# A hybrid mLSTM/GLA decoder block on one Trainium2 core: selectors made a head ahead, two products of a pair exchanged after plain units, a weights' cast behind two bank copies, a last norm in three vector steps

## The chip, the core and the metric

The kernel runs on one core of one Trainium2 chip. The metric is the device time of one execution in microseconds (us). TensorE (PE) multiplies, VectorE (DVE) and ScalarE (ACT) do the elementwise work, GpSimd (POOL) issues accumulating DMAs and SyncE (SP) most of the other DMAs. Each engine works through a list of its own, in the order in which the program wrote it; semaphores hold an instruction until what it reads, or the buffer that it writes, is ready.

## The reference

The input is x (512 tokens, width 1024), ahead of which 16 meta tokens are put. Cut to what matters:

```python
xn = rmsnorm(h, norm1_g)
(mq, mk, mv, mi, mf, mo, gq, gk, gv, ga, gr, gate_m, gate_g) = split_cols(xn @ w_in)
mq, mk = split(silu(causal_depthwise_conv(concat(mq, mk))))       # width 4
# mLSTM, 4 heads: wts = exp(dmat - m_row) * (q k^T);  dmat from sums of log gates
hm = (wts @ v) / maximum(abs(sum(wts)), exp(-m_row))
y_m = head_rmsnorm(hm) * sigmoid(mo)
y_g = head_rmsnorm(gla(gq, gk, gv, log_sigmoid(ga @ g_a2))) * silu(gr)
merged = sigmoid(gate_m) * (y_m @ w_branch_m) + sigmoid(gate_g) * (y_g @ w_branch_g)
h = h + merged @ w_out
hn = rmsnorm(h, norm2_g)
h = h + (silu(hn @ w_ff_gate) * (hn @ w_ff_up)) @ w_ff_down
out = rmsnorm(h, final_g)
```

## The kernel before

**Units.** Activations are held transposed, features on the 128 partitions and tokens along a row. The weights are cut into units of 128 output features. Every float32 operand is split into a high part, a cast (weights: `whi`, on ACT, L190), and the rest (`wlo`, on DVE, L195), and a product takes three matmuls: high by high, high by low, low by high (L304, L305, L306 in `mm3`). A plain unit has 8 steps (k) of three matmuls for each bank of PSUM; there are eight banks, which go round.

**Mixed pairs.** Most of the units are computed two at a time with seven half-size products in place of eight (a Strassen-Winograd scheme; `pair` and `seven`, matmuls L346 to L348, 12 for a product). A pair accumulates in three banks, bx, by and bz. Product p7 goes to bz; q1 goes to bx and q6 is added on top of it, then come p4, p2 and q5, and p3 is left pending into the next pair. `sink_of` names the copies that ACT makes in between: s1 copies what bx holds after q1 (before: L406), s7 copies bz after p7 (L409), s2 copies bx after q6 (L407), L408 is a copy of a pair before it. q6 writes bx, so its first matmul can't start until s1 has read it.

**Tables.** The casts for later units are hooked to steps of a unit or pair: `PLAIN`, `FIRST` (the first of two items that a pair makes) and `SECOND`. An entry such as `("q1", 2)` means: after step 2 of q1.

**The order around the units.** The program is written in one order, by hand: after each step of a unit (every second step of a product) `tick()` lets the generators that wait in `side` and the first one of `mixers` go on by one step; `yield n` makes a generator wait n ticks. The four mLSTM heads (`mlstm`) are such generators, in `mixers`, one after the other. A head begins with a selector, `sel`, a 128x256 cast of constants (L883), waits 6 ticks, and multiplies its two halves with the gate rows `gts.R` (L886, L887). The results are copied and masked (L890 and L891), ACT takes exponentials (L134, in `act`), and for each of five chunks PE makes the scores (L908 to L910), DVE multiplies them with the exponentials (L915), ACT casts the product (`wh`, L919) and DVE keeps the rest (`wl`, L928). Then come sums with the values (L950 to L956) and the head's norm (`head_out`).

**Where things meet.** The units of the four heads come first (gates, then mq, mk, mv, mo for each head, all plain; convolutions of mq and mk run on DVE and ACT beside them). Head 0's selector is made while the convolutions of head 1's mq and mk are under way. The first mixed pair is that of gm units 0 and 1, behind the last mo unit. Two other pairs follow plain units: that of gq and gk of head 1 behind the bm units, and the first fg/fu pair behind six plain fg and fu units. `mixed_x` makes the sums of activations that the pairs need (L546, L551, L582) ahead of the first pair.

**The end.** `final` makes the last norm of each half of the tokens: a sum of squares over the features by a matmul with ones (L1495), `y` = exp(-0.5 ln(...)) on ACT, and one Newton step for it on DVE (L1501 to L1504).

Of the kernel before, what the change touches and what calls it, by code (L numbers as in the profile page):

```python
# [9 lines left out]
F32R = mybir.dt.float32r  # L10
I32 = mybir.dt.int32
AF = mybir.ActivationFunctionType
ALU = mybir.AluOpType
PSUM = bass.MemoryType.PSUM

P = 128
D = 1024
KT = 8
NM = 16
NS = 512  # L20
NT = NM + NS
HALF = NT // 2
H = 4
DFF = 2816
FT = DFF // P
EPS = 1e-6
# [76 lines left out]
def hybrid_block(ctx: ExitStack, tc: tile.TileContext, xT, wst, par, con, out):  # L103
# [5 lines left out]
    def nm(s):  # L109
        cnt[0] += 1  # L110
        return f"{s}_{cnt[0]}"
# [6 lines left out]
    def tt(dt=F32, n=NT, p=P):  # L118
        t = tpool.tile([P, TW], dt, tag="t", name=nm("t"))
        return t[:p, :n]  # L120
# [7 lines left out]
    def act(o, i, func, **kw):  # L128
        want = TABLE.get(func)
        if want is not None and table[0] not in want:  # L130
            table[0] = want[0]
            if func != AF.Silu:
                S.preload_act_table_set(want[0])
        S.activation(o, i, func, **kw)  # L134
# [122 lines left out]
    def g_lo(u):  # L257
# [6 lines left out]

    PLAIN = {"s": [(split_hi, 2), (split_lo, 4)], "e": [(e_hi, 1), (e_lo, 3), (s2, 4)],
             "a": [(a_hi, 1), (a_lo, 3), (f_hi, 4), (s4, 5)]}
    FIRST = {"s": [(split_hi, ("q1", 2)), (split_lo, ("p3", 1))],
             "e": [(e_hi, ("q1", 2)), (e_lo, ("p3", 1)), (s2, ("q6", 1))]}
    SECOND = {"s": [(split_hi, ("p2", 0)), (split_lo, ("p2", 2))],
              "a": [(a_hi, ("p2", 0)), (a_lo, ("p2", 2)), (f_hi, ("q5", 0)), (s4, ("q5", 2))],  # L270
              "e": [(e_hi, ("p2", 0)), (e_lo, ("p2", 2)), (s2, ("q5", 2))]}
# [22 lines left out]
    pend = {}  # L294
# [45 lines left out]
    def seven(o, w, x, n, start, hook, c0, c1):  # L340

        wh, wl = w[n]
        xh_, xl_ = x[n]
        for k in range(4):
            h, l = wh[:, k * P:(k + 1) * P], wl[:, k * P:(k + 1) * P]
            T.matmul(o, h, xh_[k][:, c0:c1], start=start and k == 0, stop=False, skip_group_check=not start)  # L346
            T.matmul(o, h, xl_[k][:, c0:c1], start=False, stop=False, skip_group_check=not start)  # L347
            T.matmul(o, l, xh_[k][:, c0:c1], start=False, stop=k == 3, skip_group_check=not start)  # L348
            hook(n, k)

    def pair(names, x, cols, sink):


        u, steps = begin(*names)
        w = mixw[u].w
        bz, bx, by = (bank()[:, :cols[1] - cols[0]] for _ in range(3))
        e = sink(bz, bx, by)
        todo = {("p7", 0): ["s5"], ("p7", 2): ["mid", "c22"], ("q6", 0): ["c12"], ("q6", 2): ["fin"]}
        mine = {("p3", 0): ["s1", "s7"], ("p4", 0): ["s2"], ("p2", 1): ["c21"], ("q5", 0): ["c11"]}
        steps.setdefault(("p7", 3), []).append(lambda: f_lo(u))  # L360
        steps.setdefault(("q6", 1), []).append(lambda: g_hi(u))
        steps.setdefault(("p4", 1), []).append(lambda: g_lo(u))

        def hook(n, k):
            left(*todo.get((n, k), ()))
            for s in mine.get((n, k), ()):
                e.pop(s)()
            for f in steps.get((n, k), ()):
                f()
            if k % 2:  # L370
                tick()

        seven(bz, w, x, "p7", True, hook, *cols)
        seven(bx, w, x, "q1", True, hook, *cols)
        if "p3" in pend:
            pend.pop("p3")(hook)
        else:
            for k in range(4):
                hook("p3", k)
        seven(bx, w, x, "q6", False, hook, *cols)  # L380
        seven(bz, w, x, "p4", False, hook, *cols)
        seven(by, w, x, "p2", True, hook, *cols)
        seven(bx, w, x, "q5", False, hook, *cols)
        assert not pend, pend
        pend.update(e)
        pend["p3"] = lambda hook=lambda n, k: None: seven(bx, mixw.pop(u).w, x, "p3", False, hook, *cols)
# [36 lines left out]
    for k in range(KT):  # L423
        t = tt()
# [201 lines left out]
    gts = Box()  # L626
    gts.ready = False

    def gate_rows(ps):
        a2s = gts.a2s = apool.tile([P, 512], F32R, name="a2s")  # L630
        a2f = pr[:, C_A2:C_A2 + 512]
        gsb = tt()
        for a in range(2):
            c = slice(a * HALF, (a + 1) * HALF)
            V.tensor_tensor(gsb[:96, c], ps[0][a][:96], rstd[:96, c], ALU.mult)
        yield 16
        gam = gts.gam = tt(F32R)
        S.copy(gam[:96], gsb[:96])
        bi = pr[0:32, C_BG:C_BG + 1]
        bf = pr[32:64, C_BG:C_BG + 1]  # L640
        r1, r2, bl, a0 = tt(p=32), tt(p=32), tt(p=32), tt(p=32)
        act(r1, gsb[32:64], AF.Abs, bias=bf)
        yield 1
        act(r1, r1, AF.Exp, scale=-1.0)
        V.tensor_scalar(r2, gsb[32:64], bf, 0.0, op0=ALU.add, op1=ALU.min)
        yield 1
        act(r1, r1, AF.Ln, bias=b_one[:32])
        V.tensor_tensor(gam[64:96], gsb[64:96], gam[64:96].bitcast(F32), ALU.subtract)
        S.copy(a2s[:96], a2f[:96])
        yield 1  # L650
        V.tensor_tensor(r2, r2, r1, ALU.subtract)
        V.tensor_tensor_scan(bl, rmask[:32], r2, 0.0, ALU.mult, ALU.add)
        yield 1
        V.tensor_tensor(a2s[32:64], a2f[32:64], a2s[32:64].bitcast(F32), ALU.subtract)
        V.scalar_tensor_tensor(a0, gsb[0:32], bi, bl, ALU.add, ALU.subtract)
        yield 1
        d0, ml = r1, r2
        V.memset(d0, 0.0)
        V.tensor_copy(d0[:, CH::CH], bl[:, CH - 1:NT - 1:CH])
        V.tensor_tensor_scan(ml, d0, a0, 0.0, ALU.add, ALU.max)  # L660
        yield 1
        R = gts.R = tt(F32R, NS)
        mr = tt(p=32)
        rhi = d0
        act(R[0:32], ml[:, NM:], AF.Copy, scale=-1.0)
        V.tensor_tensor(mr, ml, bl, ALU.add)
        V.tensor_scalar(mr, mr, -1.0, 40.0, op0=ALU.mult, op1=ALU.min)
        yield 1
        V.scalar_tensor_tensor(R[32:64], ml[:, NM:], -1.0, R[0:32].bitcast(F32), ALU.mult, ALU.subtract)
        S.copy(R[64:96], mr[:, NM:])  # L670
        yield 1
        S.copy(rhi[:, NM:], R[64:96].bitcast(F32))
        yield 1
        V.tensor_tensor(R[96:128], mr[:, NM:], rhi[:, NM:], ALU.subtract)

        acol = gts.acol = apool.tile([P, 480], F32, name="acol")
        gts.idx = {}
        rows = [a0]
        n_ix = 0
        for d in range(NCK):  # L680
            if d > 0:
                nxt = tt(p=32)
                for i in range(NCK - d):
                    e = CH * (i + d) - 1
                    V.tensor_scalar(nxt[:, CH * i:CH * i + CH], rows[-1][:, CH * i:CH * i + CH], bl[:, e:e + 1],
                                    None, op0=ALU.add)
                rows.append(nxt)
            yield 2
        yield 8
        pst = bank()  # L690
        for d in range(NCK):
            n_ix = gate_cols(pst, rows, d, n_ix)
            yield 1
        yield 2
        V.tensor_copy(acol, pst[:, :480])
        gts.ready = True
# [178 lines left out]
    WTOT = off  # L875


    def mlstm(h, q, k, v, gates, dst):
        while not gts.ready or q.v is None or k.v is None:
            yield 1  # L880
        (qh, ql), (kh, kl) = q.v, k.v
        sel = mpool.tile([P, 2, P], F32R, tag="sel", name=nm("sel"))
        S.copy(sel, cn[:, NS + h:NS + 8:H].unsqueeze(2).to_broadcast([P, 2, P]))  # L883
        yield 6
        pb, pm = bank(), bank()
        T.matmul(pb, sel[:, 0], gts.R, start=True, stop=True)  # L886
        T.matmul(pm, sel[:, 1], gts.R, start=True, stop=True)  # L887
        yield 1
        nml, dia, em = tt(n=NS), tt(n=NS), tt(n=NS)
        S.copy(nml, pb)  # L890
        V.tensor_tensor(dia, pb, mask, ALU.add)  # L891
# [595 lines left out]
    def final(a, o):  # L1487
        yield 16
        ps = bank()[:, :HS]
        T.matmul(ps, ones, hsum[a].v, start=True, stop=False)  # L1490
        while o.v is None:
            yield 1
        yield from out_res(7, o.v, a * HS, (a + 1) * HS)
        yield 1
        T.matmul(ps, ones, hsum[a].w, start=False, stop=True)  # L1495
        yield 1
        y, t = tt(n=HS), tt(n=HS)
        act(y, ps, AF.Ln, bias=b_eps, scale=1.0 / D)
        act(y, y, AF.Exp, scale=-0.5)
        yield 1  # L1500
        V.tensor_tensor(t, y, y, ALU.mult)  # L1501
        V.scalar_tensor_tensor(t, ps, D * EPS, t, ALU.add, ALU.mult)
        V.tensor_scalar(t, t, -0.5 / D, 1.5, op0=ALU.mult, op1=ALU.add)
        V.tensor_tensor(y, y, t, ALU.mult)  # L1504
        yield 1
        for j in range(4):
            g = hgain[j, a]
            V.tensor_tensor(g, g, y.unsqueeze(1).to_broadcast([P, 2, HS]), ALU.mult)
            q = S if j % 2 else nc.sync
            q.dma_start(out[2 * j:2 * j + 2, :, a * HS:(a + 1) * HS].rearrange("m p n -> p m n"), g)  # L1510
            yield 1
# [110 lines left out]
```

## Time and profile before

| what | value |
|---|---|
| time, median of 3 runs | 942.75 us (942.73 to 942.78) |
| the profiled execution, its own time | 943.2 us |
| its span in the trace | 941.1 us (2.1 us lie around it) |
| TensorE (PE) busy | 917.7 us |
| VectorE (DVE) busy | 641.0 us |
| ScalarE (ACT) busy | 536.7 us |
| GpSimd (POOL) busy | 86.5 us |
| mean granted TensorE clock | 0.993 of full speed |

Busy times come from the profiled execution, whose own time is 0.45 us above the median of the runs. Matmuls overlap, so that the distance between two starts, not a matmul's own duration, is what it costs PE; the same holds to a smaller part for DVE and ACT.

### The profile page before, as it was taken

To read this page: it belongs to the slowest core of one execution; us is meant where nothing else is said; L and a number is where in the kernel's file an instruction comes from. 1 tells how busy PE (TensorE), PEld (TensorE's weight loads), DVE (VectorE), ACT (ScalarE), POOL (GpSimd) and SP (SyncE) were. 2 spreads that over 40 slices of the span, in tenths; PEclk is the share of its full clock that TensorE was granted. 3 is DMA by queue.
4 is the path that set the end of the run, shared out by engine and by line. 5 is a ranking of instruction groups with operands and counts; after the bars stand their busy time and mean duration, and the time that the engine had idled before them with its cause. 6 is when DMAs were issued, how large, how long until landed. Compare 5 with 4: busy or idle time off the path is not lost.

```text
span 941.1 us, 15476 instructions
## 1 busy us (share of the span) xinstructions
PE 917.7 (98%) x6083; PEld 843.0 (90%) x6083; DVE 641.0 (68%) x948; ACT 536.7 (57%) x947; POOL 86.5 (9%) x102
## 2 busy tenths in 40 slices
PE   6999999989999999999999999999999999999995
PEld 6989999989998899999998888888999999888885
DVE  6898776877865477777777556886767677832323
ACT  7556678779674266767774234443555555732321
POOL 0000022011100011111000000212111210000000
PEclk9999999999999999999999999999999999999998
DMA  6345465355752466565553344244887775332302
GB/s 255 111 132 164 136 141 134 71 125 123 173 143 88 114 152 163 135 139 141 134 137 90 114 141 131 86 124 116 196 187 186 190 179 148 113 108 70 112 1 89
DMA packets 48713, 124.45 MB, mean 132 GB/s; under 512 B 5377, under 2 KB 11521, under 8 KB 48641
## 3 DMA queue, kind: packets, MB, share of 16 engines
q1 hardware_dynamic: 35008, 101.32, 34.6%
q0 software_dynamic: 12544, 21.11, 14.5%
q8 instruction: 47, 0.77, 0.3%
q10 hardware_dynamic: 1088, 1.05, 0.3%
q14 instruction: 26, 0.20, 0.1%
HBM read 118.08 MB, written 5.37 MB: 131 GB/s over the span
## 4 chain that ended last, share of the span: by engine, by line
PE 88%; DVE 5%; ACT 5%; issue 1%; DMA 1%; SPq 0%; DVEq 0%; ACTq 0%
PE b L305 14%; PE b L304 14%; PE b L306 14%; PE b L346 12%; PE b L348 12%; PE b L347 12%; ACT t L134 2%; ACT whi L190 1%; DVE wlo L195 1%; PE b L1069 1%; PE b L1071 1%; PE b L1048 1%; DMA t<-xT 1%; PE b L753 1%; PE b L951 1%
## 5 line engine op out<-in xcount | busy, mean ns | idle before, releaser
L305 PE MATMUL b<-t,whi 128*128 128x512 f32 (+2 forms) x822 | 290.8, 354 | 1.1 <-DVE t L473 0.7
L304 PE MATMUL b<-t,whi 128*128 128x512 f32 (+2 forms) x774 | 274.6, 355 | 6.6 <-ACT t L134 6.6
L306 PE MATMUL b<-t,wlo 128*128 128x512 f32 (+2 forms) x774 | 271.6, 351 | 0.0
L346 PE MATMUL b<-t,whi 128*128 128x256 f32 (+1 forms) x864 | 249.6, 289 | 3.5 <-ACT t L406 2.8
L348 PE MATMUL b<-t,wlo 128*128 128x256 f32 (+1 forms) x864 | 245.3, 284 | 0.0
L347 PE MATMUL b<-t,whi 128*128 128x256 f32 (+1 forms) x864 | 244.5, 283 | 0.0
L195 DVE TENSOR_TENSOR wlo<-raw,whi 128x1024 fp32r<-128x1024 f32 x155 | 193.3, 1250 | 46.2 <-ACT whi L190 45.5
L190 ACT CAST whi<-raw 128x1024 fp32r<-128x1024 f32 x155 | 161.4, 1045 | 62.3 <-PE b L347 26.0
L305 PEld LDWEIGHTS b<-t,whi 128*128 128x128 f32 x822 | 156.4, 190 | 23.7 <-DVE t L473 1.3
L304 PEld LDWEIGHTS b<-t,whi 128*128 128x128 f32 x774 | 147.7, 191 | 26.6 <-ACT t L134 6.6
L346 PEld LDWEIGHTS b<-t,whi 128*128 128x128 f32 x864 | 164.0, 190 | 5.3 <-ACT t L406 3.8
L306 PEld LDWEIGHTS b<-t,wlo 128*128 128x128 f32 x774 | 147.3, 190 | 19.9 <-DVE wlo L195 0.3
L347 PEld LDWEIGHTS b<-t,whi 128*128 128x128 f32 x864 | 163.9, 190 | 0.4
L348 PEld LDWEIGHTS b<-t,wlo 128*128 128x128 f32 x864 | 163.7, 189 | 0.0
L134 ACT ACTIVATE t<-t 128x512 f32<-128x512 f32 (+6 forms) x140 | 80.5, 593 | 58.9 <-DVE t L1098 27.7
L185 POOL DMA_DIRECT2D raw<-wst x36 | 31.1, 864 | 358.2 <-DMA wf<-wst 86.6
L190 ACT CAST whi<-wf 128x1024 fp32r<-128x1024 f32 x36 | 37.8, 1051 | 22.6 <-PE b L347 13.5
L134 ACT ACTIVATE t<-f 128x256 f32<-128x256 f32 (+1 forms) x24 | 11.6, 482 | 61.9 <-DVE f L1469 61.9
L214 POOL DMA_DIRECT2D wf<-wst x36 | 32.1, 901 | 157.2 <-DMA wf<-wst 116.0
L195 DVE TENSOR_TENSOR wlo<-wf,whi 128x1024 fp32r<-128x1024 f32 x36 | 43.8, 1218 | 0.0
L1469 DVE TENSOR_TENSOR f<-f,b 128x512 f32<-128x512 f32 (+1 forms) x9 | 5.6, 628 | 53.6 <-PE b L306 53.6
L346 PE MATMUL b<-t,wgh 128*128 128x256 f32 (+1 forms) x144 | 40.9, 284 | 0.0
(221 smaller groups left out, 1200.6 us busy)
## 6 DMA issues: line engine op xcount, KB each, us to landing
raw<-wst SPq DMA_DIRECT2D x155, 512.0 KB, 3.7
wf<-wst SPq DMA_DIRECT2D x36, 256.0 KB, 3.2
wf<-wst POOLq DMA_DIRECT2D x36, 256.0 KB, 5.6
raw<-wst POOLq DMA_DIRECT2D x36, 256.0 KB, 4.8
t<-xT SPq DMA_DIRECT2D x8, 264.0 KB, 6.1
pos<-t SPq DMA_DIRECT2D x8, 264.0 KB, 2.5
t<-xT SPq DMA_DIRECT2D x8, 256.0 KB, 3.9
t<-neg POOLq DMA_DIRECT2D x6, 272.0 KB, 6.3
```

The costliest lines, as they stand in the source:

```text
L134: S.activation(o, i, func, **kw)
L185: G.dma_start(lr(r, 0), lr(wst[v - 1], 0), accum_op=ALU.add)
L190: S.copy(t, src)
L195: V.tensor_tensor(t, src, hi.bitcast(F32), ALU.subtract)
L214: G.dma_start(lr(st.f, 1), lr(wst[u + 1], 1), accum_op=ALU.add)
L304: T.matmul(o, w_h, ah[:, c0:c1], start=first, stop=False)
L305: T.matmul(o, w_h, al[:, c0:c1], start=False, stop=False)
L306: T.matmul(o, w_l, ah[:, c0:c1], start=False, stop=last)
L346: T.matmul(o, h, xh_[k][:, c0:c1], start=start and k == 0, stop=False, skip_group_check=not start)
L347: T.matmul(o, h, xl_[k][:, c0:c1], start=False, stop=False, skip_group_check=not start)
L348: T.matmul(o, l, xh_[k][:, c0:c1], start=False, stop=k == 3, skip_group_check=not start)
L753: T.transpose(pb[:, c * P:(c + 1) * P], f[:, c * CH:(c + 1) * CH], ident)
```

## The change

Four edits.

- **Selectors.** Each head's selector is made ahead: head 0's at the end of the gate rows, the next head's right behind the two matmuls of the head before it, in one buffer. The wait of 6 ticks is gone.
- **Order of p7 and q1.** Where a pair follows plain units, and no p3 is pending, q1 comes ahead of p7. There are three such pairs.
- **FIRST.** The cast `whi` moves from step 2 of q1 to step 0 of the place of p3, behind s1 and s7; `wlo` moves from step 1 of p3 to step 3, and the sum s2 from step 1 to step 2 of q6. It concerns 36 pairs.
- **The last norm.** The sum's affine part, `x`, is computed beside ACT's two steps; three DVE steps follow in place of four.

```diff
-    FIRST = {"s": [(split_hi, ("q1", 2)), (split_lo, ("p3", 1))],
-             "e": [(e_hi, ("q1", 2)), (e_lo, ("p3", 1)), (s2, ("q6", 1))]}
+    FIRST = {"s": [(split_hi, ("p3", 0)), (split_lo, ("p3", 3))],
+             "e": [(e_hi, ("p3", 0)), (e_lo, ("p3", 3)), (s2, ("q6", 2))]}
...
-        seven(bz, w, x, "p7", True, hook, *cols)
-        seven(bx, w, x, "q1", True, hook, *cols)
+
+        for b, n in ((bz, "p7"), (bx, "q1")) if "p3" in pend else ((bx, "q1"), (bz, "p7")):
+            seven(b, w, x, n, True, hook, *cols)
...
         V.tensor_tensor(R[96:128], mr[:, NM:], rhi[:, NM:], ALU.subtract)
+        selector(0)
...
+    def selector(h):
+        gts.sel = mpool.tile([P, 2, P], F32R, tag="sel", name=nm("sel"), bufs=1)
+        S.copy(gts.sel, cn[:, NS + h:NS + 8:H].unsqueeze(2).to_broadcast([P, 2, P]))
+
     def mlstm(h, q, k, v, gates, dst):
...
-        sel = mpool.tile([P, 2, P], F32R, tag="sel", name=nm("sel"))
-        S.copy(sel, cn[:, NS + h:NS + 8:H].unsqueeze(2).to_broadcast([P, 2, P]))
-        yield 6
+        sel = gts.sel
         pb, pm = bank(), bank()
         T.matmul(pb, sel[:, 0], gts.R, start=True, stop=True)
         T.matmul(pm, sel[:, 1], gts.R, start=True, stop=True)
         yield 1
+        del sel
+        if h < H - 1:
+            selector(h + 1)
...
-        y, t = tt(n=HS), tt(n=HS)
+        y, t, x = tt(n=HS), tt(n=HS), tt(n=HS)
         act(y, ps, AF.Ln, bias=b_eps, scale=1.0 / D)
+        V.tensor_scalar(x, ps, D * EPS, -0.5 / D, op0=ALU.add, op1=ALU.mult)
         act(y, y, AF.Exp, scale=-0.5)
         yield 1
         V.tensor_tensor(t, y, y, ALU.mult)
-        V.scalar_tensor_tensor(t, ps, D * EPS, t, ALU.add, ALU.mult)
-        V.tensor_scalar(t, t, -0.5 / D, 1.5, op0=ALU.mult, op1=ALU.add)
-        V.tensor_tensor(y, y, t, ALU.mult)
+        V.tensor_tensor(t, t, x, ALU.mult)
+        V.scalar_tensor_tensor(y, t, 1.5, y, ALU.add, ALU.mult)
```

The lines of the changed kernel are shifted: its selector cast is L882, the two matmuls L890 and L891, their copy L897, the scores L915 to L917, `wh` L926, and s1, s2 and s7 are L407, L408 and L410.

**ACT at head 0.** The first fence shows ACT's list before, the second the same stretch now, the third where the first selector's cast went. `whi` is a weights' cast, L513 (now L514) the high part of an activation, L134 an activation function, `sel` the selector.

```order
L134 ACTIVATE t_787<-t_777,pr 128x512
L190 CAST whi_796<-raw_625 128x1024
L513 CAST t_799<-t_775 128x528
L134 ACTIVATE t_802<-t_775 128x272
L883 CAST sel_807<-cn 128x256
L757 CAST t_835<-b_824 128x512
```

```order
L134 ACTIVATE t_789<-t_779,pr 128x512
L190 CAST whi_798<-raw_627 128x1024
L514 CAST t_801<-t_777 128x528
L134 ACTIVATE t_804<-t_777 128x272
L882 CAST sel_820<-cn 128x256
L897 COPY t_822<-b_809 128x512
L134 ACTIVATE t_824<-b_810,cb 128x512
```

```order
L134 ACTIVATE t_552<-t_487 32x512
L671 CAST t_552<-t_553 32x512
L673 COPY t_486<-t_552 32x512
L882 CAST sel_581<-cn 128x256
L190 CAST whi_587<-raw_401 128x1024
```

In the place of head 0's selector now stands that of head 1, and the copies of head 0's two products (L897 and the L134 on bank 810) come directly behind it. The first selector stands 17 rows earlier.

**ACT at the first mixed pair.** The first fence is ACT's list before, around the pair's s1 and s7 (L406, L409); the second is the list now, where they are L407 and L410. `acol` marks the exponentials of head 3, `wh` its casts; the operands `b_` are banks.

```order
L890 COPY t_2347<-b_2337 128x512
L190 CAST whi_2356<-raw_2141 128x1024
L134 ACTIVATE t_2349<-b_2338,cb 128x512
L406 COPY t_2311<-b_2307 128x256
L409 COPY t_2312<-b_2306 128x256
L134 ACTIVATE t_2372<-t_2348,acol 128x112
L134 ACTIVATE t_2372<-t_2347,acol 128x128 x2
```

```order
L926 CAST wh_2196<-t_2301 128x272
L134 ACTIVATE t_2338<-t_2174,acol 128x16
L759 CAST t_2359<-b_2346 128x512
L134 ACTIVATE t_2373<-t_2175,acol 128x16
L926 CAST wh_2196<-t_2338 128x144
L776 CAST t_1800<-b_2379 128x256
L133 ACT_TABLE_LOAD
L134 ACTIVATE t_2400<-b_2213 128x512
L134 ACTIVATE t_2401<-b_2304 128x512
L926 CAST wh_2196<-t_2373 128x16
L407 COPY t_2391<-b_2387 128x256
L410 COPY t_2392<-b_2386 128x256
```

Before, head 3 had only its two products behind it when s1 came, and all of its exponentials and `wh` casts stood behind s7. Now the whole of them stand ahead of s1: L897 of head 3 is ACT's row 223, s1 is row 268, and the 44 rows between hold head 3's exponentials, all five `wh` casts, two table loads, three weights' casts and the casts and copies of `mixed_x`. The weights' cast L190 that stood ahead of s1 stands behind L410.

**PE at the first mixed pair.** The fence shows three places of PE's list now: the pair's beginning, the step from q1 to p7, and the step from p7 to q6. Bank 2387 is bx, 2386 is bz.

```order
L773 MATMUL b_2379<-pr,t_2220 128x128
L346 MATMUL b_2387<-t_2265,whi_2318 128x256
...
L348 MATMUL b_2387<-t_2269,wlo_2330 128x256
L346 MATMUL b_2386<-t_1806,whi_2228 128x256
...
L348 MATMUL b_2386<-t_1810,wlo_2249 128x256
L346 MATMUL b_2387<-t_1996,whi_2344 128x256
```

Before, the pair began with p7 into bz, and q1 into bx stood directly ahead of q6, with three score matmuls of head 3 between. Now the 12 matmuls of p7 lie between q1 and q6, and the two selector matmuls of head 3, which stood behind the pair's p7 at row 1195, stand at row 1107, 95 rows ahead of the pair.

## Rows read from the trace of the kernel before

**Rows 1.** The page: busy time, share of the span and instructions.

```profile
PE 917.7 (98%) x6083; PEld 843.0 (90%) x6083; DVE 641.0 (68%) x948; ACT 536.7 (57%) x947; POOL 86.5 (9%) x102
```

**Rows 2.** The list of PE's waits: total, times, longest, in us.

```profile
PE b L346 <- ACT t L406: 2.8, 2, 2.3
PE b L886 <- ACT sel L883: 2.2, 1, 2.2
...
PE b L346 <- ACT t L1391: 0.5, 1, 0.5
```

**Rows 3.** Timeline of ACT at head 0's selector: start, duration, line, operation, idle before.

```profile
67.78 0.81 ACT L134 ACTIVATE t<-t,pr 128x512 f32<-128x512 f32 x1 [0.89 <-DVE t L595]
68.50 1.03 ACT L190 CAST whi<-raw 128x1024 fp32r<-128x1024 f32 x1
...
70.30 0.39 ACT L883 CAST sel<-cn 128x256 fp32r<-128x256 f32 x1
```

**Rows 4.** Timeline of PE at the same place.

```profile
70.74 0.50 PE L886 MATMUL b<-t,sel 128*128 128x512 f32 x1 [2.21 <-ACT sel L883]
```

**Rows 5.** Windows behind two waits: busy by engine (PE, PEld, DVE, ACT, POOL), then granted clock.

```profile
71.00:75.00 4.00, 4.00 (x20) 3.91 (x20) 4.00 (x8) 0.44 (x2) 0.00 (x0) 0.57 0.53 166
211.00:215.00 4.00, 4.00 (x22) 4.00 (x22) 3.56 (x7) 3.63 (x8) 0.87 (x1) 0.57 0.56 111
```

**Rows 6.** Timeline of PE: q6 of the second pair, and of the first fg/fu pair.

```profile
209.86 0.39 PE L346 MATMUL b<-t,whi 128*128 128x256 f32 x1 [2.32 <-ACT t L406]
...
650.30 0.39 PE L346 MATMUL b<-t,whi 128*128 128x256 f32 x1 [0.52 <-ACT t L1391]
650.52 0.28 PE L347 MATMUL b<-t,whi 128*128 128x256 f32 x1
650.64 0.28 PE L348 MATMUL b<-t,wlo 128*128 128x256 f32 x1
```

**Rows 7.** Timeline of ACT ahead of the second pair's s1.

```profile
208.22 1.03 ACT L190 CAST whi<-raw 128x1024 fp32r<-128x1024 f32 x1
...
209.46 0.35 ACT L406 COPY t<-b 128x256 f32<-128x256 f32 x1
```

**Rows 8.** Timeline of PE in a plain unit with 512 columns.

```profile
176.44 0.39 PE L304 MATMUL b<-t,whi 128*128 128x512 f32 x1
176.67 0.39 PE L305 MATMUL b<-t,whi 128*128 128x512 f32 x1
```

**Rows 9.** Timeline of ACT: kinds of work that stand ahead of the first s1 now.

```profile
180.02 1.20 ACT L546 CAST t<-t 128x544 fp32r<-128x544 f32 x2
...
181.60 1.39 ACT L582 CAST t<-t 128x272 fp32r<-128x272 f32 x4
...
200.04 1.28 ACT L133 ACT_TABLE_LOAD   x1
201.33 0.63 ACT L134 ACTIVATE t<-t 128x512 f32<-128x512 f32 x1
201.87 0.60 ACT L919 CAST wh<-t 128x512 fp32r<-128x512 f32 x1
202.38 0.69 ACT L134 ACTIVATE t<-t,acol 128x128 f32<-128x128 f32 x2
202.98 0.62 ACT L134 ACTIVATE t<-t 128x512 f32<-128x512 f32 x1
```

**Rows 10.** Timeline of DVE: kinds of work that stand between head 3's products.

```profile
206.02 0.69 DVE L832 SCALAR_TENSOR_TENSOR t<-t,t 128x512 f32<-128x512 f32 x1
...
207.12 0.74 DVE L839 SCALAR_TENSOR_TENSOR t<-t,halfg,t 128x512 f32<-128x512 f32 x1
...
208.11 1.22 DVE L195 TENSOR_TENSOR wlo<-wf,whi 128x1024 fp32r<-128x1024 f32 x1
```

**Rows 11.** Timeline of DVE in the last norm.

```profile
933.70 0.43 DVE L1502 SCALAR_TENSOR_TENSOR t<-b,t 128x256 f32<-128x256 f32 x1
934.16 0.29 DVE L1503 TENSOR_SCALAR t<-t 128x256 f32<-128x256 f32 x1
```

## The prediction, made before the changed kernel had run

> **What bounds the kernel now.** I read the page first: PE is busy 98% of the span [rows 1], so time can only be won where PE waits or where its clock is low. The list of PE's waits says where this change can reach [rows 2]: 2.2 us for the selector, 2.8 us for two s1 copies of pairs (2.3 the longest) and 0.5 us for an s1 copy of the first fg/fu pair. That is 5.5 us. Then I looked at windows behind the two long waits: each is followed by four microseconds in which the granted clock is 0.57 on the mean [rows 5], a stretch at 1.2 GHz with edges at 2.4. 4 x (1 - 0.57) = 1.7 us of PE's work is lost in each, which no list of waits shows. Behind the 0.5 us wait the matmuls step at 0.12 us again at once [rows 6], full speed. So a long wait costs its own length and 1.7 us more.
>
> Last I looked at ACT's timeline ahead of each wait. None is a wait for a slow copy. At head 0 the selector begins at 70.30 because an activation, held 0.89 us by DVE, and a weights' cast of 1.03 us stand ahead of it [rows 3], while PE stands still until 70.74 [rows 4]. At the second pair the copy begins at 209.46 behind a weights' cast [rows 7], and PE goes on at 209.86 after 2.32 us [rows 6].
>
> **Selectors at head 0.** The 2.2 us wait goes, since the first selector is cast some 17 instructions earlier. Behind it something else is late: the two banks of the products must be read out. The exponential on the second stands in ACT's list behind the same activation and weights' cast, then a selector (0.3 us), a copy and itself (0.5 and 0.6, as the 512-column activations of [rows 9]): 70.30 + 0.3 + 0.5 + 0.6 = 71.7. PE, which stopped at 68.5, has about 15 more matmuls of 264 columns (0.12 us each) and three of a score to do before it needs that bank, and reaches it near 70.4: a wait of 1.3 us. Three shorter ones for vector results (banks read by the convolutions, the gate columns) I put at 1.1 us together, an estimate from the order, between 0 and 2. In sum 2.4 us of waits in four pieces for 2.2 in one. What is won is the clock, 1.7 us, if none of the pieces lets it fall: a wait of 0.5 us didn't, one of 2.2 did, and 1.3 lies between. I take no fall: 2.2 + 1.7 - 2.4 = **1.5 us won**, and none if it falls.
>
> **q1 ahead of p7.** s1 may now run while PE does p7, 12 matmuls x 0.12 = 1.4 us. The copy itself takes 0.35 us [rows 7], so at the pairs behind bm and behind fu, where ACT has nothing else ahead of it, the wait of 0.5 us each is covered: **1.0 us won** (0.5 of it is the row in the list with L1391, 0.5 the shorter of the two with L406). The low parts that q1 needs are made before the pair begins at both places.
>
> **The weights' cast behind the copies.** At the pairs in the middle of the mixed stretches the list of waits has nothing, so moving a cast gives nothing; its weights are for the next item, and some 60 matmuls (7 us) of cover lie behind it. I cost it at nothing. Without that cover it would be 1 us a pair, over 36 pairs, but the 7 us are more than the cast (1.03) and the `wlo` (1.22 [rows 10]) together.
>
> **The last norm.** One step of the chain of four goes, with `x` beside ACT: the steps are 0.46 and 0.29 to 0.46 us [rows 11]: **0.3 us won**, 0.46 at most.
>
> **Head 3 and the first pair.** This is where I expect the gain to go. With 6 ticks less for each head, and heads one after the other, head 3's products come some 90 matmul rows earlier. Before, its exponentials and `wh` casts stood behind the first pair's s1, and the long wait at the second pair (2.32 us, and 1.7 us of clock) came from them. Now all of them stand ahead of the first pair's s1, with `mixed_x`'s casts. I take the two selector matmuls of head 3 as a common point, since ACT can't copy what they have not made.
>
> PE from there to q6, its first matmul that needs s1: 125 matmuls, 55 with 512 columns (0.23 us [rows 8]), 24 with 264, 24 with 256, and 22 smaller (0.12 [rows 6]): 12.7 + 8.4 = 21.1 us. In this stretch no PE wait is in the list, and I foresee one of 0.15.
>
> ACT from there to the end of s1: ten copies, casts and activations of 512 columns at 0.54 (5.4), ten exponentials of 128 columns at 0.30 (3.0), five of 16 at 0.2 (1.0, an estimate), five `wh` casts, 1344 columns where 512 take 0.51, and a fixed part (1.6), a pair of bank copies (0.5), three weights' casts at 1.03 less some overlap, 0.95 (2.85), two casts at 0.55 (1.1), eight small copies at 0.34 (2.7), one of 256 columns (0.3), two table loads at 1.28 (2.55) [rows 9], s1 itself (0.35): 21.4 us with no idle moment. So ACT, with no wait at all, would be level with PE. But it must wait. The small copies of `mixed_x` wait for the sum over head 2 (L818), which PE reaches 9.4 us behind the common point, when ACT has done 7.3; the rest is 14.1 and ends at 23.5. That gives PE a wait of 2.4 us at least. Then the `wh` casts of 272 and 144 columns wait for DVE, which has 11 instructions from the `wlo` that follows ACT's second weights' cast to the product of 144 columns: one `wlo`, four of 512 columns (0.69), two of 0.74 [rows 10], four narrower that I scale to 1.6: 7.1 us, less about 0.08 us of overlap each, 6.2 us; ACT has only 3.5 us of work in that time. 2.7 us more: s1 ends at 26.2 to 27, PE waits 5 to 6. I take **5.5 us, and 0.2 for the `wlo` of q1**, which is needed 1.4 us earlier than it was. Bounds are 2.4 (DVE never late) and 7. Behind such a wait the clock falls: 1.7 us as behind the two shorter ones, and perhaps a second such spell; I take 2.0.
>
> On the table loads a page of the Trainium skill differs. "ScalarE: Activation LUTs", section "What ACT_TABLE_LOAD costs", puts a drain of about 1.38 us behind the 1.28 us of every switch. Here the load takes 1.28 us, and the next activation begins 1.29 us after its start [rows 9], so this trace shows none. By the page the two loads would cost ACT 2.8 us more, and PE's wait would be 8.3 us.
>
> Won at the two first pairs: 0.3 us at the first q6 (a gap too short for the list), 2.3, and 1.7 of clock: 4.3. Lost: 5.5 + 0.2 + 2.0 = 7.7. **Net 3.4 us lost.** After it ACT and PE start level, and PE has 15 us of work to the second pair's q6, ACT 8.
>
> **Sum.** -1.5 - 1.0 - 0.3 + 3.4 = +0.6 us on the profiled execution's own 943.2 us, 943.8; on the median of the runs (0.45 lower) **943.4 us**. That is within 0.2% of before, 1.9 us, which is about what a measurement of this kernel can tell from no change.
>
> **The rivals.**
> - *ACT keeps up.* If the exponentials and casts of head 3 slip in between without a wait of over 1 us (ACT's 21.4 us against PE's 21.1 speaks for it; the wait for L818 against it), then there is no fall of the clock either: 942.75 - 1.5 - 1.0 - 0.3 - 4.3 + 0.8 = 936.5.
> - *DVE is never late, only ACT.* The wait is 2.4 us, the fall 1.7: 942.75 - 7.1 + 2.4 + 0.2 + 1.7 = 940.0.
> - *The clock falls at head 0 too* (slower). Four waits in about 6 us, the longest 1.3: if PE is granted 0.57 over 4 us again, then 1.7 us are lost and head 0 gives nothing: 943.4 + 1.7 = 945.1. It decides when the longest wait nears the 2.2 us that did it [rows 4, 5]. The Trainium skill, "TensorE: Matmul & The Clock Gate", section "A second HAM failure mode: psum-queue depth-cycling", tells of a kernel in which many short idle times of PE between groups on the banks sufficed; the trace here has only single waits, so no run yet shows it.
> - *A longer wait at the first pair* (slower). At 7 us with two spells of the low clock it is 942.75 - 7.1 + 7 + 0.2 + 3.4 = 946.3.
>
> **How the numbers follow.** Chances: the forecast 0.42, ACT keeps up 0.16, DVE never late 0.17, the clock at head 0 0.13, the longer wait 0.12. The forecast's own range, from a wait of 4.5 to 6.5 and a clock term of 1.7 to 2.5, is 942.1 to 944.9. The range takes in the 940.0 and the 945.1, most of the 946.3 and half of the 936.5: 937 to 946.3. Slower by over 0.2% is over 944.6: most of the last two cases and a fifth of the forecast, 0.32. Faster is under 940.9: the first two rivals, little less, 0.32. The rest, 0.36, is within 0.2%.
>
> **What would show it.** In the list of PE's waits of the changed kernel: no row for a selector; for s1 (now L407) one wait of 4 to 7 us near 197, none at the second pair, none behind bm and fu; at 63 to 72 some waits of at most 1.3 us with ACT's exponential and DVE's results as releasers, and a granted clock of 1.00 in 71 to 75. At the first pair the chain should go through DVE's product of 144 columns, ACT's cast of it, a table load and s1. The last DVE steps should end 0.3 us earlier behind ACT's last exponential. The prediction is wrong if the wait at the first q6 is under 2 us or over 7, or if a head's other matmuls wait for DVE over 1 us: the den of head 0 near 97 us is the one that I am least sure of, at up to 1.2 us.

## The result, and the profile after

Three of the changed kernel's four executions took 948.39, 949.02 and 949.70 us at a mean granted clock of 0.992; the fourth took 1175.11 us at 0.72 and is left out from here on (the median of all four is 949.36). The median of the three, 949.02 us, stands against 942.76 us for the kernel before in the same comparison: the ratio is 1.0065, with a 95% interval of 1.0046 to 1.0085. So it is slower by 6.3 us, more than the 0.6 forecast and past the range's end at 946.3. The profiled execution took 949.7 us with a span of 947.6, 6.5 us over that of before.

The list of PE's waits of the changed kernel (total, times, longest, in us) answers to [rows 2]:

```profile
PE b L304 <- ACT t L134: 7.9, 2, 6.8
PE b L346 <- ACT t L407: 5.2, 1, 5.2
PE b L346 <- ACT t L408: 2.1, 1, 2.1
...
PE b L963 <- DVE t L948: 0.7, 1, 0.7
PE b L348 <- DVE wlo L195: 0.5, 2, 0.3
PE b L891 <- DVE t L618: 0.4, 1, 0.4
PE b L346 <- DVE t L922: 0.3, 1, 0.3
...
PE b L915 <- DVE t L596: 0.3, 1, 0.3
```

L407 is s1 now, L408 is s2. Of the first row, 6.8 us is the kernel's start, where 6.6 stood before; the other 1.1 us is a wait at head 0. The selector's 2.2 us, the 2.3 us at the second pair and the 0.5 us waits behind bm and fu are gone. In their place stand 5.2 us for one s1 and 2.1 us for one s2. PE's timeline says where:

```profile
64.37 0.50 PE L891 MATMUL b<-t,sel 128*128 128x512 f32 x1 [0.36 <-DVE t L618]
67.75 0.50 PE L915 MATMUL b<-t,t 128*128 128x512 f32 x1 [0.26 <-DVE t L596]
72.09 0.39 PE L304 MATMUL b<-t,whi 128*128 128x264 f32 x1 [1.12 <-ACT t L134]
98.39 0.50 PE L963 MATMUL b<-t,onesr 128*128 128x512 f32 x1 [0.66 <-DVE t L948]
203.58 0.58 PE L346 MATMUL b<-t,whi 128*128 128x256 f32 x1 [5.18 <-ACT t L407]
...
239.03 0.39 PE L346 MATMUL b<-t,whi 128*128 128x272 f32 x1 [2.14 <-ACT t L408]
```

203.58 is the first pair's q6, where the forecast put 5.5 us. 239.03 is the third pair (gq and gk of head 0), at a matmul that writes bx again after s2 has read it. The forecast had nothing there. The windows behind both, and behind head 0's waits (us, busy of PE, PEld, DVE, ACT, POOL, then the granted clock), answer to [rows 5]:

```profile
202.00:209.00 7.00, 5.42 (x26) 5.42 (x27) 3.89 (x7) 4.27 (x11) 1.72 (x2) 0.52 0.56 93
239.00:243.00 4.00, 3.97 (x19) 3.97 (x20) 4.00 (x8) 2.84 (x7) 0.00 (x0) 0.57 0.24 98
...
72.00:76.00 4.00, 3.90 (x30) 3.91 (x31) 4.00 (x9) 2.14 (x8) 0.00 (x0) 1.00 0.47 131
```

At head 0 the clock stays up. Behind the 5.2 us wait PE worked 5.42 us at 0.52, which is 2.6 us of work lost; behind the 2.1 us wait it is 4 x 0.43 = 1.7 again.

ACT's timeline ahead of the first pair's s1 shows the chain that the forecast had worked out:

```profile
176.33 0.59 ACT L897 COPY t<-b 128x512 f32<-128x512 f32 x1 [0.67 <-PE b L890]
...
185.55 0.74 ACT L583 CAST t<-t 128x272 fp32r<-128x272 f32 x2 [1.69 <-PE b L818]
...
189.86 1.28 ACT L133 ACT_TABLE_LOAD   x1
191.16 0.63 ACT L134 ACTIVATE t<-t 128x512 f32<-128x512 f32 x1
...
196.68 0.42 ACT L926 CAST wh<-t 128x272 fp32r<-128x272 f32 x1 [0.60 <-DVE t L922]
...
200.18 0.31 ACT L926 CAST wh<-t 128x144 fp32r<-128x144 f32 x1 [2.19 <-DVE t L922]
200.40 0.37 ACT L776 CAST t<-b 128x256 fp32r<-128x256 f32 x1
200.78 1.28 ACT L133 ACT_TABLE_LOAD   x1
202.07 1.08 ACT L134 ACTIVATE t<-b 128x512 f32<-128x512 f32 x2
203.05 0.21 ACT L926 CAST wh<-t 128x16 fp32r<-128x16 f32 x1
203.14 0.39 ACT L407 COPY t<-b 128x256 f32<-128x256 f32 x1
```

The waits stand in brackets: 1.69 us for L818 on PE, then 0.60 and 2.19 us for DVE's products, then five more instructions before s1. From the common point (L890 at 175.90 on PE) to s1's end at 203.53 are 27.6 us; the forecast had 26.2 to 27.

At the third pair the same engine is late a second time:

```profile
231.14 0.63 ACT L134 ACTIVATE t<-t 128x512 f32<-128x512 f32 x1
231.68 0.36 ACT L407 COPY t<-b 128x256 f32<-128x256 f32 x1
231.93 0.38 ACT L410 COPY t<-b 128x256 f32<-128x256 f32 x1
232.19 1.06 ACT L190 CAST whi<-raw 128x1024 fp32r<-128x1024 f32 x1
233.14 1.18 ACT L134 ACTIVATE t<-t 128x512 f32<-128x512 f32 x2
...
236.26 1.28 ACT L133 ACT_TABLE_LOAD   x1
237.56 1.15 ACT L134 ACTIVATE t<-t 128x512 f32<-128x512 f32 x2
238.61 0.37 ACT L408 COPY t<-b 128x272 f32<-128x272 f32 x1
```

Between s7 (L410) and s2 (L408) ACT is never idle. The cast that FIRST moved stands there, at 232.19, with two steps of head 3's norm (the first of the group of 233.14, and another at 234.21; a third, at 231.14, is ahead of s1) and a table load. s2's source was done at 236.9, when PE stopped. PE has three products of the pair, 36 matmuls, between the start of q6 and the matmul that waits for s2.

The same stretch of ACT's list was as long before. From the start of s1 to that of s2 (then L406 and L407) ACT took 6.9 us at the third pair, and from 231.68 to 238.61 it takes 6.9 us now. But before, PE's products of head 3 with the values stood beside it. The first two rows are s1 and s2 before; the others are the first and the last of those products, before (L950, L952) and now (L957, L959):

```profile
221.51 0.40 ACT L406 COPY t<-b 128x256 f32<-128x256 f32 x1
228.41 0.38 ACT L407 COPY t<-b 128x272 f32<-128x272 f32 x1
222.89 0.39 PE L950 MATMUL b<-wh,t 128*128 128x512 f32 x1
229.25 0.26 PE L952 MATMUL b<-wh,t 128*128 128x16 f32 x1
210.90 0.39 PE L957 MATMUL b<-wh,t 128*128 128x512 f32 x1
217.16 0.26 PE L959 MATMUL b<-wh,t 128*128 128x16 f32 x1
```

### The profile page after: what moved, and what is told of

It reads as the page before. It is cut to its first block, busy times and chain, and to the rows that moved or that the text cites. A ratio compares the mean times of both kernels' runs of the same rounds, so it can differ in the third digit from the quotient of the medians.

```text
span 947.6 us, 15473 instructions
## 1 busy us (share of the span) xinstructions
PE 919.5 (97%) x6083; PEld 844.5 (89%) x6083; DVE 640.6 (68%) x948; ACT 534.2 (56%) x946; POOL 87.0 (9%) x102
## 4 chain that ended last, share of the span: by engine, by line
PE 86%; DVE 6%; ACT 6%; issue 1%; DMA 1%; SPq 0%; DVEq 0%; ACTq 0%
PE b L304 14%; PE b L305 14%; PE b L306 14%; PE b L346 12%; PE b L348 12%; PE b L347 12%; ACT t L134 2%; DVE wlo L195 1%; ACT whi L190 1%; PE b L1076 1%; ACT L133 1%; PE b L1078 1%; PE b L1055 1%; DMA t<-xT 1%; PE b L958 1%
## 5 line engine op out<-in xcount | busy, mean ns | idle before, releaser
L306 PE MATMUL b<-t,wlo 128*128 128x512 f32 (+2 forms) x774 | 270.8, 350 | 0.0
L190 ACT CAST whi<-raw 128x1024 fp32r<-128x1024 f32 x155 | 162.1, 1050 | 57.1 <-PE b L347 24.5
L306 PEld LDWEIGHTS b<-t,wlo 128*128 128x128 f32 x774 | 146.7, 190 | 19.9 <-DVE wlo L195 0.3
L134 ACT ACTIVATE t<-t 128x512 f32<-128x512 f32 (+5 forms) x140 | 80.4, 594 | 59.8 <-DVE t L1105 27.5
L190 ACT CAST whi<-wf 128x1024 fp32r<-128x1024 f32 x36 | 37.9, 1052 | 22.6 <-PE b L347 12.8
L214 POOL DMA_DIRECT2D wf<-wst x36 | 35.0, 979 | 154.9 <-DMA wf<-wst 91.3
L134 ACT ACTIVATE t<-f 128x256 f32<-128x256 f32 (+1 forms) x24 | 11.6, 484 | 61.7 <-DVE f L1476 61.7
L1398 ACT COPY t<-b 128x256 f32<-128x256 f32 x48 | 16.4, 375 | 44.0 <-PE b L348 44.0
```

What stands on the lines that cost most here:

```text
L190: S.copy(t, src)
L214: G.dma_start(lr(st.f, 1), lr(wst[u + 1], 1), accum_op=ALU.add)
L306: T.matmul(o, w_l, ah[:, c0:c1], start=False, stop=last)
L1398: s7=lambda: S.copy(s[:, lo], bz), s1=lambda: S.copy(s[:, hi], bx), s2=lambda: S.copy(r[:, lo], bx),
```

## The experiments

Each is timed against the kernel before on the same chip; every interval is at 95%. Unless it is said otherwise, a cut of code shows the edit against the changed kernel, and `...` stands for lines left out.

**Only the selectors' edit** (the other three edits undone):

```diff
 (selectors ahead, no wait of 6 ticks, as in the change)
-    FIRST = {"s": [(split_hi, ("p3", 0)), (split_lo, ("p3", 3))],
-             "e": [(e_hi, ("p3", 0)), (e_lo, ("p3", 3)), (s2, ("q6", 2))]}
+    FIRST = {"s": [(split_hi, ("q1", 2)), (split_lo, ("p3", 1))],
+             "e": [(e_hi, ("q1", 2)), (e_lo, ("p3", 1)), (s2, ("q6", 1))]}
...
-        for b, n in ((bz, "p7"), (bx, "q1")) if "p3" in pend else ((bx, "q1"), (bz, "p7")):
-            seven(b, w, x, n, True, hook, *cols)
+        seven(bz, w, x, "p7", True, hook, *cols)
+        seven(bx, w, x, "q1", True, hook, *cols)
...
 (last norm in four steps)
```

> Only the selectors' edit, without the wait of 6 ticks; pairs, FIRST and the last norm as before. Theory 1 (the heads come too early: ACT and DVE carry head 3's work into the first and third pair): at least as slow as the full change, about 950 to 952 us, with a wait of 5 to 6.5 us at the first pair's q6 and a second wait of over 1 us with a low clock at the third pair. Theory 2 (the moved cast of FIRST delays s2, and the third pair's loss of some 4 us is its doing): about 945 to 946, with the first pair's wait and none at the third.

Measured: 950.38 us, ratio 1.0081 (1.0065 to 1.0098). This edit alone loses 7.7 us, no less than the full change; the two intervals overlap. PE's timeline:

```profile
204.34 0.58 PE L346 MATMUL b<-t,whi 128*128 128x256 f32 x1 [6.08 <-ACT t L406]
233.18 0.39 PE L346 MATMUL b<-t,whi 128*128 128x272 f32 x1 [1.03 <-ACT t L406]
239.17 0.39 PE L346 MATMUL b<-t,whi 128*128 128x272 f32 x1 [1.20 <-ACT t L407]
```

With the cast ahead of s1, the first wait is 0.9 us longer than the 5.18. At the third pair two waits stand, one for s1 and one for s2, where the full change has one of 2.14. Theory 1 holds in this: ACT is late there without the moved cast too. The low clock that it named for the third pair did not come: the granted clock is 1.00 in 233 to 237 and in 239 to 243.

**The full change without the selectors' edit:**

```diff
-        selector(0)
...
-        sel = gts.sel
+        sel = mpool.tile([P, 2, P], F32R, tag="sel", name=nm("sel"))
+        S.copy(sel, cn[:, NS + h:NS + 8:H].unsqueeze(2).to_broadcast([P, 2, P]))
+        yield 6
```

> The full change without the selectors' edit: products exchanged, cast moved, last norm in three steps. Theory 1: the long waits are those of before (2.2 at the selector, about 2.3 at the second pair), the three small gains stay: 941.3 to 942.2 us. Theory 2: the third pair loses 2 to 4 us here too: 943.5 to 946.

Measured: 940.47 us, ratio 0.9975 (0.9966 to 0.9984): 2.2 us faster than before, a little more than expected. The selector's wait is back, with 2.22 us, and the second pair's stands in two parts:

```profile
208.76 0.39 PE L346 MATMUL b<-t,whi 128*128 128x256 f32 x1 [1.36 <-ACT t L407]
215.79 0.39 PE L346 MATMUL b<-t,whi 128*128 128x256 f32 x1 [2.00 <-ACT t L408]
```

No wait is left at the first and at the third pair. So the change's loss hangs on the selectors' edit.

**The full change with FIRST as before:**

```diff
-    FIRST = {"s": [(split_hi, ("p3", 0)), (split_lo, ("p3", 3))],
-             "e": [(e_hi, ("p3", 0)), (e_lo, ("p3", 3)), (s2, ("q6", 2))]}
+    FIRST = {"s": [(split_hi, ("q1", 2)), (split_lo, ("p3", 1))],
+             "e": [(e_hi, ("q1", 2)), (e_lo, ("p3", 1)), (s2, ("q6", 1))]}
```

> The full change with FIRST as before. Theory 1: 948 to 950.5 us, the first pair's wait about 1 us longer than the 5.2 of the full change, since the cast stands ahead of s1 again, and a wait remains at the third pair. Theory 2: 944 to 946, no wait of over 0.5 us at the third pair.

Measured: 947.5 us, ratio 1.0055 (1.004 to 1.007), 1.5 us less than the full change. Neither theory foresaw that. PE's waits at the first and the third pair, and the windows behind those of the third:

```profile
203.53 0.58 PE L346 MATMUL b<-t,whi 128*128 128x256 f32 x1 [6.14 <-ACT t L407]
232.23 0.39 PE L346 MATMUL b<-t,whi 128*128 128x272 f32 x1 [1.03 <-ACT t L407]
238.22 0.39 PE L346 MATMUL b<-t,whi 128*128 128x272 f32 x1 [1.20 <-ACT t L408]
```

```profile
232.00:236.00 4.00, 3.77 (x30) 3.78 (x31) 1.87 (x3) 3.98 (x9) 1.11 (x2) 1.00 0.96 198
238.00:242.00 4.00, 3.78 (x28) 3.60 (x29) 4.00 (x9) 3.30 (x8) 0.00 (x0) 1.00 0.01 1
```

The cast ahead of s1 costs 1 us more at the first pair. At the third pair PE waits 2.2 us in either case; but here it is in two waits six microseconds apart, and the granted clock reads 1.00 behind both, where the full change's one wait of 2.14 is followed by 0.57. By the traces, the moved cast so wins 1 us at the first pair and loses 1.7 us of clock at the third, 0.7 of the 1.5 us. The times do not settle it. The intervals of the two overlap, and one of the four executions here has the mean granted clock of the full change (0.992, the three others 0.994) and took 948.48 us, inside the full change's 948.39 to 949.70. That the low clock is the moved cast's doing is not shown.

**The full change with the 6 ticks kept**, so that heads stay where they were:

```diff
         sel = gts.sel
+        yield 6
         pb, pm = bank(), bank()
```

> The full change, but the heads keep their wait of 6 ticks; the selector alone is made ahead. Theory 1: head 0's wait and its low clock go (2.2 + 1.7, less some 0.3 for bank waits), heads stay where they were, small gains of 1.3: 937.5 to 939 us; the 2.3 us at the second pair may stay. Theory 2: the cast still costs at the third pair: 940 to 943.

Measured: 940.01 us, ratio 0.998 (0.9971 to 0.9989): faster than before by 2.7 us, but 1 to 2.5 us short of what theory 1 expected. PE's timeline shows what it missed:

```profile
69.59 0.50 PE L892 MATMUL b<-t,sel 128*128 128x512 f32 x1 [1.25 <-DVE acol L697]
73.39 0.50 PE L916 MATMUL b<-t,t 128*128 128x512 f32 x1 [1.13 <-DVE t L764]
```

With the selector early, the bank of the second product and then that of the first scores are late, for DVE: 2.4 us of waits for 2.2, and only the low clock is won. At the second pair 1.40 and 1.99 us stay, as in the run without the selectors' edit.

**Head 3 alone put back.** Heads 0 to 2 stay as early as in the change:

```diff
         sel = gts.sel
+        if h == H - 1:
+            yield 24
         pb, pm = bank(), bank()
```

> The full change, but head 3 alone waits 24 ticks, which puts its two selector matmuls back behind the first pair's first product (as before); heads 0 to 2 stay early. If the place of head 3 is what costs, the first pair's 5.2 us wait and the third pair's 2.1 with their low clocks go, and the second pair waits about 1.4 and 2.0 us as with the 6 ticks: 939.5 to 941.5 us. If early heads cost wherever they are: over 944.

Measured: 938.51 us, ratio 0.9956 (0.9941 to 0.9971), 4.1 us faster than before and 10.5 below the full change. PE's list of waits:

```profile
PE b L346 <- ACT t L407: 1.0, 2, 0.6
...
PE b L965 <- DVE t L950: 0.7, 1, 0.7
```

The waits for s1 are down to 0.6 and less, and none for s2 is left. That is faster than expected: the 1.4 and 2.0 us at the second pair did not come, one wait of 0.39 stands there. So the place of head 3 alone makes the loss; heads 0 to 2 may come early for the 0.7 us of the den (L965 there) and the three short waits at head 0, which the full change has too. It beats the version with the 6 ticks, too. Two things differ there, heads 0 to 2 and head 3, which now starts 14 matmuls later than before; which of them wins was not tried.

**Only FIRST changed:**

> Only FIRST changed. The prediction put this at nothing (942.7). The runs without the selectors' edit speak for about 1 us won: the second pair's wait of 2.3 us splits into one for s1 of 1.4 and one for s2 of 2.0, and the granted clock stays up in 211 to 215: 941.3 to 942.2.

The edit is the two lines of FIRST in the change's diff. Measured: 941.86 us, ratio 0.9991 (0.9981 to 1.0). The 2.3 us wait does split into 1.37 and 1.99, and in the trace the clock stays up behind both, as expected; the interval touches 1, so the gain of 0.7 us is not certain.

**The 6 ticks kept, FIRST as before:**

> Selectors ahead with the 6 ticks kept, products exchanged, last norm in three steps, FIRST as before. If the moved cast wins about 1 us at the second pair without the early heads, this is 940.7 to 941.5, with a wait of 2.3 us and a low clock at the second pair; if it wins nothing: 940.0.

Both edits are shown above. Measured: 939.91 us, ratio 0.9974 (0.9963 to 0.9986), the same as with the cast moved. The expected wait is there, but not the low clock, in the execution that was traced:

```profile
209.78 0.39 PE L346 MATMUL b<-t,whi 128*128 128x256 f32 x1 [2.33 <-ACT t L407]
```

```profile
209.00:215.00 6.00, 4.81 (x39) 4.61 (x39) 5.49 (x11) 4.70 (x12) 0.99 (x2) 1.00 0.59 100
```

So the clock did not fall there behind a wait as long as that of [rows 6]. A wait of 1.29 us for s2 follows at 215.88; the two add up to 3.6 us, where the version with the cast moved has 3.4 in its two.

**The cast behind s2 as well** (6 ticks kept):

```diff
-    FIRST = {"s": [(split_hi, ("p3", 0)), (split_lo, ("p3", 3))],
-             "e": [(e_hi, ("p3", 0)), (e_lo, ("p3", 3)), (s2, ("q6", 2))]}
+    FIRST = {"s": [(split_hi, ("p4", 0)), (split_lo, ("p4", 2))],
+             "e": [(e_hi, ("p4", 0)), (e_lo, ("p4", 2)), (s2, ("p4", 3))]}
```

> As the version with the 6 ticks, but FIRST's cast goes to step 0 of p4, behind s2 as well. If the cast's place on ACT ahead of s2 makes the second pair's 2.0 us wait, that wait falls to about 1.0 and the time to 938.7 to 939.3; if other work ahead of s2 sets it (wh casts and exponentials of head 3), 940.

Measured: 948.77 us, ratio 1.0064 (1.0047 to 1.0081). Both expectations failed. The 2.0 us wait at the second pair stayed at 2.01, so other work sets it; and the low parts now come too late for the mixed pairs' matmuls at six places, up to 1.5 us each:

```profile
PE b L348 <- DVE wlo L195: 5.3, 6, 1.5
PE b L346 <- ACT t L408: 2.0, 1, 2.0
```

These waits, and one of 0.5 us for the low part of a plain unit (L306, at 497.41), give 5.8 of the 8.8 us that it is slower than with the cast at p3; where the rest lies is open. It shows that the cover of the moved cast, which I had put at 7 us for all pairs, is much thinner at some.

**Head 3 put back, FIRST as before:**

> The version with head 3 alone put back by 24 ticks, with FIRST as before. It tells what the moved cast does where head 3's work stands behind the first s1. If the cast is worth something only where ACT is overloaded by head 3: 938.3 to 939, like the 938.5 with the cast moved. If it spares a wait with a low clock at the second pair: 939.5 to 941, with a wait of about 2 us there.

Measured: 939.65 us, ratio 0.997 (0.9958 to 0.9981), 1.1 us above the version with the cast moved, though the intervals of the two overlap. Its waits for s1 are 0.78, 0.78, 0.63 and 1.36 us (at 194.86, 207.69, 219.26 and 236.51), against 0.39 and 0.61: the cast, 1 us of ACT's time, stands ahead of s1 again. No low clock was needed for it. The time lies in the second of the two ranges, but without the wait of 2 us that it was to come from.

**Head 3 put back and head 0's den 6 ticks later** (the cut shows the edit against the version with head 3 put back):

```diff
-            yield 24
+            yield 18
...
         V.tensor_tensor(dl, es, dh.bitcast(F32), ALU.subtract)
-        yield 6
+        yield 12 if h == 0 else 6
```

> The version with head 3 put back, and head 0's sum over its weights (the den) 6 ticks later, head 3's own wait shortened by as many. The 0.7 us wait of the den near 98 goes: 937.6 to 938.2 us. If the 6 ticks move heads 1 and 2 into a worse place instead: over 938.5.

Measured: 937.57 us, ratio 0.995 (0.9936 to 0.9963), the fastest median, though its runs (936.83 to 938.52) reach those of the one before. The wait of the den is gone; waits of 1.57 us for s1 and 0.50 for a low part came in at the first pair, where head 3 stands 12 matmuls earlier.

**Only the exchange of q1 and p7:**

> Only the exchange of q1 and p7 after plain units. As predicted: two waits of 0.5 us for s1 go, behind bm and behind fu; the place behind bm gets a wait of about 0.2 for q6's low part instead: 0.7 to 1.0 us won, 941.7 to 942.1 where before is 942.7. If ACT or DVE are late for the exchanged product: 942.7 or more.

Measured: 941.09 us, ratio 0.9985 (0.9976 to 0.9994): 1.4 us won, with an interval that holds the predicted 1.0. The two 0.5 us waits are not in its list. One that was expected at 0.2 us behind bm is not either: it shows only where the cast is moved as well (0.19 us at 349.28 in the full change). In its place the first pair waits 0.50 us for a low part, at 195.37.

**Only the last norm:**

> Only the last norm in three steps. As predicted: 0.3 us won between ACT's last exponential and the last DVE products, 942.3 to 942.6 where before is 942.7; the interval may hold no change.

Measured: 942.1 us, ratio 0.9996 (0.9987 to 1.0004). By time alone it can't be told from nothing. In its trace the exponential's start and the last products' start, 932.52 and 934.35, are 1.83 us apart, as in the full change (939.67 and 941.50); they were 932.79 and 934.95 before, 2.16 us: 0.33 us, as predicted.

## Why the prediction was wrong

The terms of its sum against the profiled executions:

| term | forecast | found |
|---|---|---|
| head 0: selector's wait and clock, less new waits | -1.5 | -2.2 (2.2 + 1.7 gone; 0.36 + 0.26 + 1.12 come) |
| q1 ahead of p7 | -1.0 | -1.0, and 0.2 for a low part behind bm (with the moved cast) |
| last norm | -0.3 | -0.33 |
| first two pairs | +3.4 | +4.1 (5.2 + 0.6 + 2.6 for 2.3 + 0.3 + 1.7) |
| den of head 0 | 0, up to 1.2 | +0.7 |
| third pair | 0 | +3.8 (2.1 + 1.7) |

That makes 5.3 of the 6.5 us; the rest lies in pieces of some 0.1 to 0.3 us, such as the longer step behind each wait and 0.14 at the start, which are not resolved here.

**The step that failed** is the one that closes the paragraph on head 3: "After it ACT and PE start level, and PE has 15 us of work to the second pair's q6, ACT 8." That was true, and the second pair has no wait. But I stopped there and did not follow head 3 to the third pair. Before, PE's products of head 3 with the values, 30 matmuls and the two of the den, stood in the third pair and gave ACT time: from 222.89 to 229.25 in the trace of before. Now they stand at the end of the first pair and the beginning of the second, between 210.90 and 217.16, and steps of the norm that follows from them are on ACT when the third pair needs s1 and s2. ACT's stretch from s1 to s2 is no longer than before, 6.9 us; what is gone is PE's work beside it. In place of the nothing that the forecast had, the third pair waits 2.1 us and loses 1.7 us of clock. The run with the selectors' edit alone has waits there too, 1.03 and 1.20 us, and the run with head 3 put back has none: the place of head 3 as their cause is shown. Which of ACT's instructions there would have to go was not tried.

**The second error** is "I cost it at nothing", of the moved cast. The cover that I named lies ahead of the next use of its weights. I did not ask what it is put in front of: s2. With early heads, the cast joins two waits of about 1.1 us into one of 2.1, and in the trace the clock falls: 947.5 us without it, 949.02 with it, a difference that the intervals do not make certain. Without early heads it costs nothing and may win: 0.7 us alone, 1.1 with head 3 put back, nothing with the 6 ticks; none of the three is clear of the noise. And its cover was thinner than 7 us, as the run with the cast at p4 showed.

**What was right.** The first pair: q6 waits 5.2 us where 5.5 were forecast, through L818 (1.69 us, forecast 2.1) and DVE's two products (0.60 and 2.19, forecast 2.7 together). The nearness of the two numbers is in part luck: from the common point to its stop at q6 (198.40) PE took 22.5 us, forecast 21.1, and ACT took 27.6, forecast 26.2 to 27, so that two errors of the same sign cancel. Head 0: a longest wait of 1.12 us, forecast 1.3, for the exponential on the second bank, with no fall of the clock. The rival with the low clock at head 0 did not happen: the granted clock reads 1.00 behind its three waits, and behind the two of 1.25 and 1.13 us with the 6 ticks. So nothing here shows the failure of short idle times that the Trainium skill, "TensorE: Matmul & The Clock Gate", section "A second HAM failure mode: psum-queue depth-cycling", tells of. The table load's price was right as read from the row: 1.28 us, and the next activation starts 1.30 us after the load's start (189.86 and 191.16), so the drain that "ScalarE: Activation LUTs" of the Trainium skill adds in "What ACT_TABLE_LOAD costs" isn't seen in this trace either.

**Of the sizes**, the clock behind the long wait cost 2.6 us against 2.0. The two rivals on the fast side, by which ACT or DVE would have kept up, are out.

## What to carry to other kernels

Where generators run one after the other, ticks taken out of each add up: the last one moves by all of them, and what counts is which stage its work now falls into, on each engine. Add up the engine's queue from a point that both engines must pass, as was done here for the first pair, and go on until the moved work has left the list; stopping at the first place where the engines are level hid 3.8 us of this loss. And for an instruction that is moved, ask what stands behind it in its new place, not only what needs its result.

## What the runs showed of the hardware

The length of a wait alone does not tell whether the clock falls. In the kernel before, a wait of 2.32 us is followed by 0.57 [rows 5, 6]; in the version with the 6 ticks and FIRST as before, a wait of 2.33 us for the same s1 is followed by 1.00 over 209 to 215. Waits of 1.99 to 2.01 us at the second pair (four versions) had no low clock behind them, the third pair's 2.14 had. What PE did before these waits differs between the versions; what of it decides was not tried.

Nor does the program alone tell. With only FIRST changed, four of ten executions had a mean granted clock of 0.997 and took 940.44 to 940.86 us; the other six had 0.993 to 0.995 and took 941.86 to 942.87. The traced one is of the second kind (0.995): its clock is low behind head 0's wait of 2.22 us and in the last norm, and nowhere else. A difference of 0.002 over 940 us is about the 1.7 us of one such stretch, so the four had probably none at head 0. One trace shows one execution, and a low clock in it is not yet a property of the kernel.

The low clock by the 5.2 us wait lasted longer than the others. It is under 1.00 in eight windows of one microsecond in a row, from 201 to 209, and began while PE still waited; behind the waits of 2.2, 2.3 and 2.1 us it is so in four (71 to 75 and 211 to 215 before, 239 to 243 now).
